# Low halves of weight tiles by an accumulating DMA instead of a VectorE subtraction

## The chip, the cores and the metric

The kernel runs on one core of one Trainium2 chip. The metric is the device time of one execution in microseconds. Three runs of the kernel before took 1213.09, 1211.47 and 1210.93 us; the median is 1211.47 us. In the profile the engines are called PE (TensorE), DVE (VectorE), ACT (ScalarE), POOL (GpSimd) and SP (SyncE, which issues most DMAs here).

## The reference

One decoder block on 512 tokens, to which 16 meta tokens are prepended (528 rows), with a model width of 1024:

```python
h = h + 0.5 * swiglu(rmsnorm(h, ffn1_norm), ffn1_w_gate, ffn1_w_up, ffn1_w_down)   # 1024 -> 2816 -> 1024
u = rmsnorm(h, mix_norm)
c_q, c_kv, k_rope, g_q, g_k, g_v, g_b, g_a, g_z, gate_mla, gate_gdn = split(u @ w_in)
y_mla = mla(c_q, c_kv, k_rope, ...) @ w_mla_o           # latent attention, 8 heads
y_gdn = gated_deltanet(g_q, g_k, g_v, ...) @ w_gdn_o    # short convolution, chunked delta rule
h = h + (sigmoid(gate_mla) * y_mla + sigmoid(gate_gdn) * y_gdn) @ w_out
h = h + 0.5 * swiglu(rmsnorm(h, ffn2_norm), ffn2_w_gate, ffn2_w_up, ffn2_w_down)
return rmsnorm(h, final_norm)[:, N_META:]
```

All of it is in float32.

## The kernel before, in words

**Products in halves.** PE multiplies in a reduced form of float32 (`fp32r`). To keep the precision, each operand is split into a high half, which is the value rounded to that form, and a low half, which is the difference. `mm3` (L182) makes a product of three passes: high weight by high data, high weight by low data, low weight by high data.

**Weight tiles.** `weights` (L178) and `wtiles` (L168) load a tile of 128 x 1024 float32 (512 KB; 128 x 768 for the down projection's last chunk) into `wraw` from SP's queue (3 buffers), cast it on ACT into `whi` (L173), and subtract on DVE into `wlo` (L174), 3 buffers each. There are 127 such tiles: 12 gate or up tiles of each feed-forward's first part, 24 down tiles (`wd`) of each, 36 of the mixer's projection (`win`), one for `ukv`, two for `uq`, and eight each of the merge's `mo` and `wo`.

**The two feed-forwards.** The first six column tiles of the gate and up matrices are multiplied directly ("gu", L188). The other 16 go in blocks of two by two with seven products instead of eight (`quad`, L405 and L421): their operands are sums of raw blocks (`sf`), each split on ACT and DVE into a `form` tile (L272, L273). Form tiles take their buffers in turn from the pools `whi`, `wlo` and `wex`. The hidden part is cut into three chunks of 8, 8 and 6 tiles; while a chunk is multiplied by the gate and up matrices, the down products ("dn") of the chunk before are put between the quads, so that down tile and seven sub-products alternate. The last chunk's eight down tiles follow one after another.

**The mixer** (374 to 764 us in the profile) has the projections, the triangular systems of the delta rule, the scan and the attention interleaved by slots (`At`), with eight heads of small matmuls. **The merge** multiplies by `mo` (gates applied on DVE, added on POOL as `sg`, L1326, then split on ACT and DVE into `mhl`, `mhA`, `mhD`) and then by `wo`. Feed-forward 2 and the last norm end the kernel.

**What sets the order.** The code is written in program order with priorities (`At`, `cur_priority`), and a scheduler with a model of costs sets the order of each engine's instructions; buffers of the pools and semaphores do the rest. Each engine, and each DMA queue's issuing engine, runs its instructions in that order.

Of the kernel before, what the change touches and what calls it, by code (L numbers as in the profile page):

```python
# [9 lines left out]
F32 = mybir.dt.float32  # L10
F32R = mybir.dt.float32r
AF = mybir.ActivationFunctionType
ALU = mybir.AluOpType
# [4 lines left out]
P = 128  # L18
# [4 lines left out]
KT = D // P  # L23
# [26 lines left out]
}.items() for n in ns.split()}  # L50
SOLVE = 16
M34 = 17.5
WLO = ()
LAG = 3
NC1 = 3
NC2 = 3
# [5 lines left out]
NSF = 3  # L62
ORD = (2, 0, 3, 1, 4, 5, 6, 7)
ONP = (2, 3)
NFORM = {"whi": 3, "wlo": 3, "wex": 2}
CYCLE = (0, 1, 2)
HOLD = (('nm', 0, 0, 32), ('nm', 1, 0, 36), ('b', 0, 1, 36), ('g', 0, 2, 42), ('tok', 1, 4, 5), ('tok', 2, 5, 4), ('tok', 3, 6, 2), ('back', 0, 8, 25), ('tok', 4, 8, 21), ('tok', 7, 10, 0), ('sq', 0, 11, 25), ('kvn', 0, 14, 12), ('kvn', 1, 14, 18))
GX = (1,) * 16
# [13 lines left out]
KW, VW, QW, MISC, CKV, CQ, ZW, GM, GG = 1, 5, 9, 0, 13, 14, 16, 20, 28  # L82
# [10 lines left out]
def build(tc, a, out, tap=None):  # L93
    nc = tc.nc
    ctx = ExitStack()
    tap = tap or (lambda name, ap: None)
    with ctx:
        cst = ctx.enter_context(tc.tile_pool(name="cst", bufs=1))
        wp = ctx.enter_context(tc.tile_pool(name="wp", bufs=3))
# [25 lines left out]
        def mm_tile(name):  # L125
            return mmp.tile([P, 2, 512], F32, tag="mm", name=name)
# [7 lines left out]
        def ax_tile(name):  # L134
            return smp.tile([P, 512], F32, tag="ax", name=name, bufs=1)

        table_ops, fence, last_split, trail, marks, tiles = [], [None], [], [], {}, {}

        def mark(name, i, ins):
            marks.setdefault((name, i), []).append(ins.ins)  # L140
# [18 lines left out]
        def halves(t):  # L159
            return t[:, :, 0:HALF]  # L160
# [4 lines left out]
        def v2(ap):  # L165
            return ap.rearrange("p (a b) -> p a b", a=2)

        def wtiles(src, n, pool_lo=0):  # L168
            raw = wp.tile([P, 8, P], F32, tag="wraw", name="wraw", bufs=3)
            hi = wp.tile([P, 8, P], F32R, tag="whi", name="whi")  # L170
            lo = wp.tile([P, 8, P], F32R, tag="wlo", name="wlo")
            nc.sync.dma_start(raw[:, 0:n], src)
            ih = nc.scalar.copy(hi[:, 0:n], raw[:, 0:n])  # L173
            il = (nc.gpsimd if pool_lo else nc.vector).tensor_tensor(out=lo[:, 0:n], in0=raw[:, 0:n], in1=hi[:, 0:n].bitcast(F32), op=ALU.subtract)  # L174
            last_split[:] = ih.ins, il.ins
            return hi, lo

        def weights(src, n, pool_lo=0):  # L178
            hi, lo = wtiles(src, n, pool_lo)
            return [(hi[:, i], lo[:, i]) for i in range(n)]  # L180

        def mm3(outs, ws, xs, start, stop):  # L182
# [9 lines left out]
        def outs528(ps):  # L192
            return [(ps[:, 0, 0:HALF], 0, HALF), (ps[:, 1, 0:HALF], HALF, NT)]
# [77 lines left out]
        def split(pool, x, hi, lo, eng=None):  # L271
            nc.scalar.copy(hi, x)  # L272
            (eng or nc.vector).tensor_tensor(out=lo, in0=x, in1=hi.bitcast(F32), op=ALU.subtract)  # L273
# [3 lines left out]
        def form(x, pool):  # L277
            tag = ("whi", "wlo", "wex")[CYCLE[cycle[0] % len(CYCLE)]]
            cycle[0] += 1
            t = (pool if tag == "wex" else wp).tile([P, 8, P], F32R, tag=tag, name="form", bufs=NFORM[tag])  # L280
            split(wp, x, t[:, 0:4], t[:, 4:8])
# [188 lines left out]
            for m in range(KT):  # L470
                down(len(CHUNKS) - 1, m)

        # ---------------- feed-forward 1
        xs = []
        with tc.tile_pool(name="hid", bufs=1) as hid, tc.tile_pool(name="fp", bufs=2) as fp:
            norm = Norm(fp, NT, "n1", None, nc.vector)
# [36 lines left out]
        tap("h1", h1d)  # L513


        # ---------------- token mixer
        gated = dr.tile([16, P, SEQ], F32, name="gated")
        zd = dr.tile([4, P, SEQ], F32, name="zd")
        yd = dr.tile([4, P, SEQ], F32, name="yd")
# [7 lines left out]
        win = a["win"]  # L527
# [15 lines left out]
        mixer = ExitStack()  # L543
# [5 lines left out]
        def tmp(name, n=SEQ, parts=P, dt=F32):  # L549
            tag = TAG[name]  # L550
            return mx.tile([P, NT + 3], dt, tag=tag, name=name, bufs=NTAG[tag])[0:parts, 0:n]
# [14 lines left out]

        def proj(t, name, n=NT, ax=False):
            with At(WPRI):
                w = weights(win[t], KT, t in WLO)
            if ax:  # L570
                ps = ax_tile(name)
                mm3([(ps, NM, NT)], w, us, True, True)
                return ps
            ps = mm_tile(name)
            trail.clear()
            if n == NT:
                mm3(outs528(ps), w, us, True, True)
                tiles[t] = list(trail)
                return halves(ps)
            mm3([(ps[:, 0, :], NM, NT)], w, us, True, True)  # L580
            tiles[t] = list(trail)
            return ps[:, 0, :]
# [22 lines left out]
        ktok = [tok("ktok") for c in range(5)]  # L605
        bv = [tok("bv") for c in range(5)]

        # ---- rates and decays, token-major
        def rates():
            ps = proj(MISC, "misc")  # L610
            nc.vector.tensor_tensor(out=v2(misc), in0=ps, in1=v2(r), op=ALU.mult)
# [86 lines left out]
                nc.vector.tensor_tensor(out=e1, in0=e1, in1=e2, op=ALU.add if x else ALU.subtract)  # L698
                dq.dma_start(krd[16 * x:16 * x + 16], e1)

        # ---- short convolution, token-major copies
        def conv_tile(t, ci, dst):
            ps = proj(t, "qkv")
            x = tmp("cx", NT + 3)
# [66 lines left out]
        def hs(tiles, h, lo_, hi_):  # L771
            return tiles[h // 2][64 * (h % 2):64 * (h % 2) + 64, lo_:hi_]

        # ---- the triangular systems
        def decay(c, lower, n):
            if lower:
                t = b4("dec", [P, H, P]) if c else one([NM, H, NM], "L0")
# [191 lines left out]
                nc.vector.tensor_tensor(out=zs, in0=ps, in1=zs, op=ALU.mult)  # L969
                dq.dma_start(yd[:, :, o - NM:o - NM + P].rearrange("i p t -> p i t"), zs)  # L970

        # ---- the compressed keys, values and queries
        ckvn, cqn = [], []
        cph, cpl = one([P, P], "cph", F32R), one([P, P], "cpl", F32R)

# [50 lines left out]

        def queries():
            with At(WPRI):
                wq = weights(a["uq"][:, 0:8], 8) + weights(a["uq"][:, 8:12], 4)
            ps = mm_tile("qr")  # L1030
            for x in range(2):
                mm3([(ps[:, x, :], 0, SEQ)], wq[8 + 2 * x:10 + 2 * x], cqn, True, True)
            cosq, sinq = tmp("cosq"), tmp("sinq")
            dq.dma_start(cosq, a["cosq"])
            dq.dma_start(sinq, a["sinq"])
            for x in range(2):
                e1, e2 = tmp("e1"), tmp("e2")
                nc.vector.tensor_tensor(out=e1, in0=ps[:, x, :], in1=cosq, op=ALU.mult)
                nc.vector.tensor_tensor(out=e2, in0=ps[:, 1 - x, :], in1=sinq, op=ALU.mult)
                nc.gpsimd.tensor_tensor(out=e1, in0=e1, in1=e2, op=ALU.add if x else ALU.subtract)  # L1040
                dq.dma_start(qrd[x], e1)
            for t in range(4):
                ps = mm_tile("qn")
                mm3([(ps[:, 0, :], 0, SEQ)], wq[2 * t:2 * t + 2], cqn, True, True)
                qn = tmp("qn")
                ecopy(EQ[t])(qn, ps[:, 0, :])
                dq.dma_start(qnd[t], qn)

        # ---- latent attention
        mS = one([P, NT + NM], "mS")  # L1050
        nb = one([P, H, 4], "nb")
        ls = one([P, H, 4], "ls")
# [110 lines left out]
        def gate_steps(js):  # L1163
            for j in js:
                with At(WPRI):
                    w = weights(win[GM + j], KT, GM + j in WLO)
                ps = ax_tile("gate")
                for k in range(KT):
                    mm3([(ps, NM, NT)], w[k:k + 1], us[k:k + 1], k == 0, k == KT - 1)
                    if k < KT - 1:  # L1170
                        yield
                t = tmp("gt")
                nc.vector.tensor_tensor(out=t, in0=ps, in1=r[:, NM:NT], op=ALU.mult)
                dq.dma_start(gated[j], t)
                yield
# [41 lines left out]
            for _ in gates:  # L1217
                pass

        # ---- emission; At(slot) sets the priority of a part  # L1220
        with At(0):
            rates()
        table_set(SILU)
# [27 lines left out]
        with At(10):  # L1251
            nc.vector.tensor_tensor(out=hd(bv[0][0:NM]), in0=psm[0:NM].rearrange("p c (h d) -> p (c h) d", d=64),
                                    in1=hb(beta[0:NM, 0], NM), op=ALU.mult)
# [48 lines left out]
        with At(60):  # L1302
            attention()

        # ---- merge
        table_set("sigmoid_and_others")
        tc.cur_priority = p0 + 200 * STEP
        yxs = []
# [6 lines left out]
        for m in range(KT):  # L1315
# [4 lines left out]
            w = weights(a["mo"][m], 8)  # L1320
# [14 lines left out]
        norm = Norm(mx, SEQ, "n2", True)  # L1335
# [11 lines left out]
        tap("h2", h2d)  # L1347
        mixer.close()

        # ---------------- feed-forward 2 and the last norm  # L1350
        with tc.tile_pool(name="hid2", bufs=1) as hid, tc.tile_pool(name="fp2", bufs=2) as fp:
            norm3 = Norm(fp, SEQ, "nf")
            h3 = []
# [120 lines left out]
```

## Time and profile before

| | |
|---|---|
| median of three runs | 1211.47 us (1210.93 to 1213.09) |
| span of the profiled execution | 1213.2 us |
| PE busy | 1182.6 us, 97% of the span |
| DVE busy | 857.0 us, 71% |
| ACT busy | 539.7 us, 44% |
| POOL busy | 127.1 us, 10% |
| HBM read, written | 126.47 MB, 17.55 MB |

The profile is of one execution; its span is the time from the first to the last instruction, and the busy times are sums over instructions of an engine. A busy PE is not PE at its peak, since matmuls overlap and their ends are modelled. "PEclk" is the granted TensorE clock, 1.00 for full speed. A row's bracket, as in [4.39 <-PE dn], is the time the engine was idle before it and what ended that time.

### The profile page before, as it was taken

The numbers are of one execution on the slowest core, as the hardware profiler recorded it, in microseconds if no ns is written. First come the engines' busy times: TensorE is split into PE (matmuls) and PEld (weight loads), VectorE is DVE, ScalarE is ACT, GpSimd is POOL, SyncE is SP. The second block draws the span as 40 slices with busy tenths as digits, with TensorE's granted clock in tenths as the row PEclk, the third lists the DMA queues.
The fourth block names the chain that finished last, engine by engine and source line by source line (L and its number), as shares of the span: only waits on it lengthen the run. The fifth ranks groups of instructions, "written<-read, shape, count | busy, mean of one in ns | idle before, by whom it ended". The sixth has DMA issues, their size and how long they took to land.

```text
span 1213.2 us, 20599 instructions
## 1 busy us (share of the span) xinstructions
PE 1182.6 (97%) x8094; PEld 1072.4 (88%) x8094; DVE 857.0 (71%) x1545; ACT 539.7 (44%) x922; POOL 127.1 (10%) x129
## 2 busy tenths in 40 slices
PE   7999999999999899999999999999999999999996
PEld 7999999999999789788897777788889999999985
DVE  7978777876656877784667665554979777786754
ACT  6544334533345553254425564434536433543443
POOL 1000000000011545020400000222000000000002
PEclk9999999999999888898999999999999999999998
DMA  6433233232244322245534544554642233233222
GB/s 233 143 103 100 94 105 105 88 118 75 88 138 138 126 61 81 81 145 149 162 101 142 173 132 135 169 185 141 199 157 88 90 103 104 94 106 115 79 78 70
DMA packets 68961, 145.37 MB, mean 120 GB/s; under 512 B 20000, under 2 KB 26480, under 8 KB 68864
## 3 DMA queue, kind: packets, MB, share of 16 engines
q1 hardware_dynamic: 68320, 143.52, 37.0%
q8 instruction: 64, 1.05, 0.3%
q10 hardware_dynamic: 544, 0.52, 0.1%
q14 instruction: 33, 0.27, 0.1%
HBM read 126.47 MB, written 17.55 MB: 119 GB/s over the span
## 4 chain that ended last, share of the span: by engine, by line
PE 86%; DVE 5%; issue 3%; POOL 2%; ACT 2%; DMA 2%; SPq 0%; DVEq 0%; POOLq 0%; ACTq 0%
PE gu L405 27%; PE dn L188 21%; PE gu L188 11%; PE gate L188 6%; PE wo L188 4%; PE mo L188 3%; PE qkv L188 2%; DVE wlo L174 1%; PE kk L804 1%; PE s L1085 1%; PE s L1082 1%; PE qk L943 1%; POOL rk L827 1%; DVE rk L827 1%; DVE T L829 1%
## 5 line engine op out<-in xcount | busy, mean ns | idle before, releaser
L173 ACT CAST whi<-wraw 128x1024 fp32r<-128x1024 f32 (+1 forms) x127 | 129.2, 1017 | 195.6 <-issue 65.3
L174 DVE TENSOR_TENSOR wlo<-wraw,whi 128x1024 fp32r<-128x1024 f32 (+1 forms) x127 | 155.8, 1227 | 26.2 <-ACT whi L173 25.5
L405 PE MATMUL gu<-hd,form 128*128 128x264 f32 (+1 forms) x1152 | 154.6, 283 | 0.0
L405 PEld LDWEIGHTS gu<-hd,form 128*128 128x128 f32 x1152 | 146.6, 190 | 1.3
L272 ACT CAST form<-sf 128x512 fp32r<-128x512 f32 x128 | 78.6, 620 | 126.1 <-DVE sf L394 67.5
L323 DVE SCALAR_TENSOR_TENSOR hk<-dn,hk 128x528 f32<-128x528 f32 (+2 forms) x49 | 33.7, 688 | 109.8 <-PE dn L188 109.6
L405 PE MATMUL gu<-ut,form 128*128 128x264 f32 x768 | 101.1, 284 | 0.0
L405 PE MATMUL gu<-rb,form 128*128 128x256 f32 x768 | 100.0, 283 | 0.0
L188 PE MATMUL dn<-hd,whi 128*128 128x264 f32 (+2 forms) x366 | 97.4, 319 | 0.0
L272 ACT CAST form<-wraw 128x512 fp32r<-128x512 f32 x96 | 59.3, 620 | 85.2 <-PE gu L405 52.1
L405 PEld LDWEIGHTS gu<-ut,form 128*128 128x128 f32 x768 | 96.5, 188 | 0.0
L405 PEld LDWEIGHTS gu<-rb,form 128*128 128x128 f32 x768 | 95.6, 192 | 0.0
L273 DVE TENSOR_TENSOR form<-sf,form 128x512 fp32r<-128x512 f32 x128 | 86.9, 683 | 11.2 <-ACT form L272 11.1
L188 PE MATMUL gate<-ut,whi 128*128 128x512 f32 x256 | 87.8, 417 | 0.0
L188 PE MATMUL dn<-ra,whi 128*128 128x264 f32 x464 | 85.3, 285 | 0.0
L188 PE MATMUL dn<-ut,whi 128*128 128x512 f32 (+1 forms) x238 | 83.6, 390 | 0.0
L235 POOL TENSOR_TENSOR sqa<-sq 128x512 f32<-128x512 f32 (+1 forms) x3 | 4.5, 1514 | 674.3 <-ACT sq L222 674.3
L188 PE MATMUL gu<-ra,whi 128*128 128x264 f32 x384 | 64.5, 290 | 7.4 <-ACT whi L173 6.6
L188 PE MATMUL dn<-ra,wlo 128*128 128x264 f32 x352 | 71.6, 285 | 0.0
L188 PE MATMUL dn<-ut,wlo 128*128 128x512 f32 (+1 forms) x182 | 70.4, 387 | 0.0
L273 DVE TENSOR_TENSOR form<-wraw,form 128x512 fp32r<-128x512 f32 x96 | 65.5, 684 | 6.7 <-ACT form L272 6.4
L188 PEld LDWEIGHTS dn<-ra,whi 128*128 128x128 f32 x464 | 68.5, 189 | 0.0
(435 smaller groups left out, 2480.7 us busy)
## 6 DMA issues: line engine op xcount, KB each, us to landing
wraw<-w SPq DMA_DIRECT2D x88, 512.0 KB, 3.3
wraw<-win SPq DMA_DIRECT2D x36, 512.0 KB, 3.5
wraw<-d SPq DMA_DIRECT2D x32, 512.0 KB, 3.8
wraw<-d SPq DMA_DIRECT2D x16, 384.0 KB, 3.2
hk<-xT SPq DMA_DIRECT2D x16, 264.0 KB, 3.6
dec<-growd SPq DMA_DIRECT2D x8, 512.0 KB, 5.8
gated<-gt SPq DMA_DIRECT2D x16, 256.0 KB, 2.2
sg<-gated SPq DMA_DIRECT2D x16, 256.0 KB, 2.8
```

The costliest lines, as they stand in the source:

```text
L173: ih = nc.scalar.copy(hi[:, 0:n], raw[:, 0:n])
L174: il = (nc.gpsimd if pool_lo else nc.vector).tensor_tensor(out=lo[:, 0:n], in0=raw[:, 0:n], in1=hi[:, 0:n].bitcast(F32), op=ALU.subtract)
L188: trail.append(nc.tensor.matmul(o, lhsT=w, rhs=x[:, lo_:hi_], start=start and k == 0 and pi == 0, stop=stop and k == n - 1 and pi == 2).ins)
L272: nc.scalar.copy(hi, x)
L273: (eng or nc.vector).tensor_tensor(out=lo, in0=x, in1=hi.bitcast(F32), op=ALU.subtract)
L323: nc.vector.scalar_tensor_tensor(out=o, in0=p, scalar=0.5, in1=o, op0=ALU.mult, op1=ALU.add)
L405: nc.tensor.matmul(ps, lhsT=wt, rhs=xt, start=k == 0 and i == 0, stop=k == 3 and i == 2)
L804: nc.tensor.matmul(ps[0:n, h4, 0:n], lhsT=hs(kT, h, o, o + n), rhs=hs(kT, h, o, o + n), start=True, stop=True)
L827: eng.tensor_tensor(out=tm, in0=lt[:, m + 1:m + 1 + n, m:m + 1].broadcast_to([nl, n, m + 1]), in1=T[:, m:m + 1, 0:m + 1].broadcast_to([nl, ...
L829: eng.tensor_tensor(out=T[:, m + 1:m + 1 + n, 0:m + 1], in0=T[:, m + 1:m + 1 + n, 0:m + 1], in1=tm, op=ALU.subtract)
L943: nc.tensor.matmul(ps[:, h4], lhsT=hs(kT, h, o, o + n), rhs=hs(qT, h, o, o + n), start=True, stop=True)
L1082: nc.tensor.matmul(ps[:, 0:w], lhsT=Q[h][:, b * P:(b + 1) * P], rhs=K[h][:, k0:k1], start=True, stop=True)
```

## The change

Two ways of making a tile now stand beside each other. `wtiles` is as before. In `wtiles_dma` ACT makes the high half and, in a second pass, its negative into the buffer of the low half; then POOL issues a DMA from the same place in HBM that `wraw` was loaded from, with an addition, so that the low half becomes raw minus high. The first five tiles of the program (`NEARLY`), those of `win` and `uq` (`own`), and `ukv`, which calls `wtiles` itself, stay with DVE; 83 tiles take the new path: 31 in feed-forward 1 (7 gate or up, 24 down), 16 in the merge and 36 in feed-forward 2 (12 and 24). `whi` has 4 buffers instead of 3, and `wlo` 5. The size of the scratch for DMAs whose descriptors the core itself writes is set to 4096. Names that nothing used, and comments, go.

```diff
-WLO = ()
+OWN = True
-NFORM = {"whi": 3, "wlo": 3, "wex": 2}
+NFORM = {"whi": 4, "wlo": 5, "wex": 2}
+NEARLY = 5
...
+        nw = [0]
...
-        def wtiles(src, n, pool_lo=0):
+        def wtiles(src, n):
...
-            il = (nc.gpsimd if pool_lo else nc.vector).tensor_tensor(out=lo[:, 0:n], in0=raw[:, 0:n], in1=hi[:, 0:n].bitcast(F32), op=ALU.subtract)
+            il = nc.vector.tensor_tensor(out=lo[:, 0:n], in0=raw[:, 0:n], in1=hi[:, 0:n].bitcast(F32), op=ALU.subtract)
...
-        def weights(src, n, pool_lo=0):
-            hi, lo = wtiles(src, n, pool_lo)
+        def wtiles_dma(src, n):
+            raw = wp.tile([P, 8, P], F32, tag="wraw", name="wraw", bufs=3)
+            hi = wp.tile([P, 8, P], F32R, tag="whi", name="whi", bufs=NFORM["whi"])
+            lo = wp.tile([P, 8, P], F32R, tag="wlo", name="wlo", bufs=NFORM["wlo"])
+            nc.sync.dma_start(raw[:, 0:n], src)
+            nc.scalar.copy(hi[:, 0:n], raw[:, 0:n])
+            nc.scalar.activation(lo[:, 0:n], hi[:, 0:n].bitcast(F32), AF.Copy, scale=-1.0)
+            nc.gpsimd.dma_start(lo[:, 0:n], src, accum_op=ALU.add)
+            return hi, lo
+
+        def weights(src, n, own=False):
+            hi, lo = (wtiles if own or nw[0] < NEARLY else wtiles_dma)(src, n)
+            nw[0] += 1
             return [(hi[:, i], lo[:, i]) for i in range(n)]
...
-                w = weights(win[t], KT, t in WLO)
+                w = weights(win[t], KT, OWN)
...
-                wq = weights(a["uq"][:, 0:8], 8) + weights(a["uq"][:, 8:12], 4)
+                wq = weights(a["uq"][:, 0:8], 8, True) + weights(a["uq"][:, 8:12], 4, True)
...
-                    w = weights(win[GM + j], KT, GM + j in WLO)
+                    w = weights(win[GM + j], KT, OWN)
...
-    nc = bacc.Bacc("TRN2", target_bir_lowering=False, num_devices=1)
+    nc = bacc.Bacc("TRN2", target_bir_lowering=False, num_devices=1, dynamic_dma_scratch_size=4096)
```

ACT at the first quad of feed-forward 1 that has a down tile ahead of it; `g` is the gate's activation, `whi` the down tile's high half, `p` the copy of the quad's first product. Before:

```order
L147 ACTIVATE g<-g 128x528
L272 CAST form<-sf 128x512
L272 CAST form<-wraw 128x512
L421 COPY p_1486<-gu 128x264
L173 CAST whi<-wraw 128x1024
L272 CAST form<-wraw 128x512 x2
L272 CAST form<-sf 128x512 x4
```

Now:

```order
L149 ACTIVATE g<-g 128x528
L185 CAST whi<-wraw 128x1024
L186 ACTIVATE wlo<-whi 128x1024
L434 COPY p_1494<-gu 128x264
L285 CAST form<-wraw 128x512 x2
L285 CAST form<-sf 128x512
```

The cast of the down tile has moved ahead of the copy `p`, and the negation into `wlo` stands right behind it; the copy and the casts of the forms come after both.

POOL from the end of the attention (`of` is its last multiplication for a block of queries) into the merge (`sg` is the sum of the two gated branches of tile 0, 1, 2, ...). Before:

```order
L1157 TENSOR_TENSOR of<-of,rl 128x512
L1108 MEMSET vf 32x64 x2
L1157 TENSOR_TENSOR of<-of,rl 128x512 x2
L1326 TENSOR_TENSOR sg_8503<-sg_8503,sg_8504 128x512
L1326 TENSOR_TENSOR sg_8546<-sg_8546,sg_8547 128x512
```

Now:

```order
L1170 TENSOR_TENSOR of<-of,rl 128x512
L187 DMA wlo<-mo 128x1024 x3
L1170 TENSOR_TENSOR of<-of,rl 128x512
L187 DMA wlo<-mo 128x1024
L1339 TENSOR_TENSOR sg_8534<-sg_8534,sg_8535 128x512
L187 DMA wlo<-mo 128x1024
L1339 TENSOR_TENSOR sg_8578<-sg_8578,sg_8579 128x512
L187 DMA wlo<-mo 128x1024
L1339 TENSOR_TENSOR sg_8622<-sg_8622,sg_8623 128x512
```

The DMAs for the tiles 0 to 3 of `mo` stand ahead of the first sum, and from there one DMA stands behind each sum: that of tile 4 behind the sum of tile 0, and so on into `wo`, with the DMA of `wo`'s third tile between the last two sums.

PE in the later part of the mixer (`v` and `kn` are products of the latent keys and values, `gate` a projection, `z` and `x` the small products of the triangular systems). Before:

```order
L1022 MATMUL v<-wlo,ckh 128x512
L188 MATMUL gate<-ut,whi 128x512 x2
L188 MATMUL gate<-ut,wlo 128x512
L188 MATMUL gate<-ut,whi 128x512 x2
L188 MATMUL gate<-ut,wlo 128x512
L188 MATMUL gate<-ut,whi 128x512
L864 MATMUL z_6671<-xt,dec 32x32 x32
L1022 MATMUL v<-whi,ckh 128x512
```

Now:

```order
L1035 MATMUL v<-wlo,ckh 128x512
L877 MATMUL z_6702<-xt,dec 32x32 x32
L201 MATMUL gate<-ut,whi 128x512
L201 MATMUL gate<-ut,wlo 128x512
L201 MATMUL gate<-ut,whi 128x512
L1035 MATMUL v<-whi,ckh 128x512
```

The 32 small products `z` follow the product `v` at once, and the gate's matmuls come behind them, three at a time between the products.

## Rows read from the trace of the kernel before

**Rows 1.** The page, busy time, share and instructions of each engine.

```profile
PE 1182.6 (97%) x8094; PEld 1072.4 (88%) x8094; DVE 857.0 (71%) x1545; ACT 539.7 (44%) x922; POOL 127.1 (10%) x129
```

**Rows 2.** Stretches: length, each engine's busy time, PEclk, DMA share, GB/s.

```profile
23.00:81.00 58.00, 58.00 (x482) 57.97 (x481) 50.22 (x85) 29.29 (x48) 0.00 (x0) 1.00 0.39 127
81.00:327.00 246.00, 246.00 (x2023) 246.00 (x2022) 189.28 (x338) 102.81 (x167) 0.00 (x0) 1.00 0.31 97
...
374.00:764.00 390.00, 377.16 (x2558) 321.25 (x2557) 260.79 (x548) 177.54 (x357) 76.73 (x90) 0.95 0.40 124
763.60:803.40 39.80, 39.80 (x171) 32.17 (x172) 23.33 (x28) 17.47 (x24) 12.63 (x7) 1.00 0.53 164
803.40:848.10 44.70, 44.70 (x194) 35.96 (x193) 21.16 (x25) 17.02 (x24) 12.83 (x7) 1.00 0.50 167
848.10:916.00 67.90, 67.90 (x297) 55.05 (x296) 56.03 (x92) 33.19 (x53) 0.00 (x0) 1.00 0.48 159
916.00:1155.00 239.00, 239.00 (x1679) 223.95 (x1679) 186.09 (x334) 102.78 (x167) 0.00 (x0) 1.00 0.32 100
```

**Rows 3.** PE's waits, the two longest: us in all, times, longest.

```profile
PE gu L188 <- ACT whi L173: 6.6, 1, 6.6
PE tok L723 <- ACT kT L147: 5.7, 1, 5.7
```

**Rows 4.** The chain of waits in feed-forward 1: start, length, work.

```profile
127.98 5.85 PE dn L188 x48
133.83 10.22 PE gu L405 x84
...
326.74 46.94 PE dn L188 x384
```

**Rows 5.** Groups by line and shape: busy, mean ns, idle before.

```profile
L174 DVE TENSOR_TENSOR wlo<-wraw,whi 128x1024 fp32r<-128x1024 f32 x110 | 139.1, 1265 | 26.2 <-ACT whi L173 25.5 <-PE qkv L188 0.3
...
L174 DVE TENSOR_TENSOR wlo<-wraw,whi 128x768 fp32r<-128x768 f32 x16 | 15.3, 955 | 0.0
...
L173 ACT CAST whi<-wraw 128x768 fp32r<-128x768 f32 x16 | 13.4, 836 | 41.4 <-PE dn L188 28.4 <-issue 6.6 <-PE gu L405 6.5
...
L147 ACT ACTIVATE dec<-dec 128x1024 f32<-128x1024 f32 x8 | 8.2, 1051 | 5.0 <-POOL dec L783 5.0
```

**Rows 6.** The timeline of one steady period, 148 to 163 us.

```profile
149.70 1.05 ACT L173 CAST whi<-wraw 128x1024 fp32r<-128x1024 f32 x1 [4.39 <-PE dn L188]
150.78 1.23 DVE L174 TENSOR_TENSOR wlo<-wraw,whi 128x1024 fp32r<-128x1024 f32 x1
...
155.85 0.62 ACT L272 CAST form<-wraw 128x512 fp32r<-128x512 f32 x1 [2.31 <-PE gu L405]
...
160.45 0.40 PE L188 MATMUL dn<-ra,wlo 128*128 128x264 f32 x2
```

**Rows 7.** DMA: a queue's packets, MB, share; issues' count, KB, us to landing.

```profile
q1 hardware_dynamic: 68320, 143.52, 37.0%
...
wraw<-d SPq DMA_DIRECT2D x32, 512.0 KB, 3.8
...
dec<-growd SPq DMA_DIRECT2D x8, 512.0 KB, 5.8
```

**Rows 8.** The timeline between the merge's two projections.

```profile
804.99 2.04 POOL L1326 TENSOR_TENSOR sg<-sg,sg 128x512 f32<-128x512 f32 x1 [3.39 <-DVE sg L1325]
...
808.46 0.19 PEld L188 LDWEIGHTS wo<-mhl,whi 128*128 128x128 f32 x1 [0.36 <-DVE mhl L273]
```

**Rows 9.** The later mixer: two stretches as in rows 2, and one timeline row.

```profile
480.00:570.00 90.00, 85.74 (x614) 72.10 (x613) 65.41 (x131) 39.10 (x66) 14.13 (x20) 0.91 0.36 115
550.00:560.00 10.00, 10.00 (x82) 8.14 (x82) 5.66 (x8) 4.95 (x11) 0.00 (x0) 0.55 0.34 119
...
547.90 2.11 PE L864 MATMUL z<-xt,dec 32*32 32x32 f32 x64 [0.38 <-DVE xt L856]
```

More of the change, by code (lines that the diff above doesn't have):

```diff
@@ L166, in v2 @@
             return ap.rearrange("p (a b) -> p a b", a=2)
-        def wtiles(src, n, pool_lo=0):
+        def wtiles(src, n):
             raw = wp.tile([P, 8, P], F32, tag="wraw", name="wraw", bufs=3)
-            hi = wp.tile([P, 8, P], F32R, tag="whi", name="whi")
-            lo = wp.tile([P, 8, P], F32R, tag="wlo", name="wlo")
+            hi = wp.tile([P, 8, P], F32R, tag="whi", name="whi", bufs=NFORM["whi"])
+            lo = wp.tile([P, 8, P], F32R, tag="wlo", name="wlo", bufs=NFORM["wlo"])
             nc.sync.dma_start(raw[:, 0:n], src)
             ih = nc.scalar.copy(hi[:, 0:n], raw[:, 0:n])
-            il = (nc.gpsimd if pool_lo else nc.vector).tensor_tensor(out=lo[:, 0:n], in0=raw[:, 0:n], in1=hi[:, 0:n].bitcast(F32), op=ALU.subtract)
+            il = nc.vector.tensor_tensor(out=lo[:, 0:n], in0=raw[:, 0:n], in1=hi[:, 0:n].bitcast(F32), op=ALU.subtract)
             last_split[:] = ih.ins, il.ins
             return hi, lo
-        def weights(src, n, pool_lo=0):
-            hi, lo = wtiles(src, n, pool_lo)
+        def wtiles_dma(src, n):
+            raw = wp.tile([P, 8, P], F32, tag="wraw", name="wraw", bufs=3)
+            hi = wp.tile([P, 8, P], F32R, tag="whi", name="whi", bufs=NFORM["whi"])
+            lo = wp.tile([P, 8, P], F32R, tag="wlo", name="wlo", bufs=NFORM["wlo"])
+            nc.sync.dma_start(raw[:, 0:n], src)
[6 more added lines that the diff above has]
+            nw[0] += 1
             return [(hi[:, i], lo[:, i]) for i in range(n)]
```

## The prediction

> **What bounds the kernel now.** I read the busy shares first. The PE row shows 97% of the span, DVE 71%, ACT 44% and POOL 10% [rows 1]; a lighter DVE helps only where PE waits for it. The stretches show where PE is at its limit: it is busy for the whole of 23 to 81 us and 81 to 327 us (feed-forward 1), of the two projections of the merge, and of the second feed-forward, and the granted clock is 1.00 there. In 374 to 764 us (the mixer) it is busy 377.16 of 390.00 us at 0.95 [rows 2]. Whatever time can be won beyond PE's own work lies in the mixer: 12.84 us idle and about 0.05 x 390 = 19.5 us of clock.
>
> The list of PE's waits comes next. The two longest are 6.6 us for the first high half at the start and 5.7 us for kT in the mixer [rows 3]; none of its 13 lines names a low half, which is what the change replaces. The chain of waits repeats it: in a steady period of feed-forward 1 a down tile holds PE 5.85 us and seven sub-products 10.22 us, 16.07 us together, one after the other, with no other engine between them [rows 4].
>
> **What is removed, added and moved.** 127 weight tiles are split before. 83 change path: 31 in feed-forward 1 (7 gate or up tiles after the first five, 24 down), 16 in the merge, 36 in feed-forward 2. Of the 83, 16 are the 768-wide down tiles of the last chunks, 67 are 1024 wide.
>
> *DVE* loses 67 x 1.265 + 16 x 0.955 = 84.8 + 15.3 = 100.0 us [rows 5]: 857 becomes about 757 us, 62%. On PE's path none of this lies, so I count it at 0.
>
> *ACT* gains one pass for each. The nearest operation of the same kind, size and engine is the activation on dec, 1.051 us; for 768 columns I take the cast, 0.836 us [rows 5]. 67 x 1.051 + 16 x 0.836 = 83.8 us, so 540 becomes about 624 us, 51%. What stands behind it on ACT is the next p copy and the casts of the forms, 1.05 us later. In the steady period ACT idles 2.31 us, waiting for a buffer that PE still reads, before the cast at 155.85 [rows 6]; this takes the delay up. If that cover were gone in each of the 32 periods with such a tile (16 in each feed-forward), the price would be at most 32 x 1.05 = 34 us; none of PE's 13 waits names a form, so I take 0.
>
> *SP's queue* keeps all its loads. The raw tile is free after ACT's cast and no longer after DVE's pass, 1.26 us sooner (150.75 against 152.01 [rows 6]); its next load starts so much sooner, which nobody waits for. *POOL* gets 83 issues; in the feed-forward's quads it has no work of its own, 0.00 us in 81 to 327 [rows 2]. *DMA* has 83 more reads of the same weights: 67 x 0.524 + 16 x 0.393 = 41.4 MB, on 143.52 MB [rows 7].
>
> **The new wait: low half by DMA.** In the steady period the high half is cast from 149.70 to 150.75, DVE's low half is ready at 152.01, and PE wants it at 160.45 [rows 6]: 8.44 us early. Now the negation ends at about 151.80 and 8.65 us are left for issue and landing. No DMA issued by POOL and no accumulating one is in this trace, so both parts need bounds. Landing: 3.8 us, as the plain load of the same 512 KB for a down tile, up to 5.8 us, the longest median of a 512 KB transfer (dec) [rows 7]. Issue on POOL: 0 up to 2.04 us, a whole pass of POOL over half such a tile [rows 8]. The sum is 3.8 to 7.84 us, and 0.8 to 4.9 us of the 8.65 stay. I take the nearer row, 3.8, and 1 us for the issue; the cost to PE is 0 at either end.
>
> In the dense phases there is no quad between tiles, but the high half has four buffers instead of three, so that a tile may be cast three tiles ahead. The shortest tile is the 768-wide one: 46.94 us / 384 matmuls = 0.122 us, times 36, 4.40 us [rows 4]. Three of these are 13.2 us; less cast and negation (0.84 each), 11.5 us are left for the DMA. In the merge a tile takes 39.80 / 171 x 24 = 5.59 us, so more.
>
> **POOL's queue in the merge.** From the order of POOL, the DMA for the low half of mo tile m + 4 stands behind the addition sg of tile m, in order. For the last tile it ends at 807.03 [rows 8], 3.6 us after the tile's matmuls, which end with the stretch at 803.4 [rows 2]; tile m + 4 starts three tiles, 16.8 us, after tile m ends, so 13 us are left for issue and landing. The other way, POOL's work waits for issues. The one addition without slack is the last: PE waits 0.36 us for the product made from it, at 808.46 [rows 8]. One issue stands between sg 6 and sg 7, but POOL idles 3.39 us ahead of sg 7, so an issue of up to that is hidden. On the other side, DVE's low half that ran beside sg 7 is gone, which can bring back at most 0.36 us. I take 0.
>
> **DMA engines.** 143.52 MB in 37.0% of 1213.2 us is 320 GB/s with all engines busy [rows 1, 7], so a 512 KB tile is 1.64 us of all 16. In a steady period the share goes from 0.31 to (0.31 x 16.07 + 1.64) / 16.07 = 0.41. In the first projection of the merge it goes from 0.53 x 39.8 = 21.1 us by 7.1 tiles x 1.64 = 11.7 to 32.8 of 39.8 us; in the second from 22.4 by 13.1 to 35.5 of 44.7; at the start of feed-forward 2 from 0.48 x 67.9 = 32.6 by 12 tiles, 19.7, to 52.3 of 67.9 [rows 2]. It fits, at 0.77 to 0.83. The cost is 0 as long as the accumulating transfer costs the engines what a plain one costs.
>
> **The mixer.** Its projections stay on the old path. Up to about 480 us the order of DVE, ACT and PE is that of before. After that PE's order differs. The 32 small matmuls z of the last merging step before the scan's end, which waited 0.38 us for DVE's transpose xt at 547.90 [rows 9], stood behind seven gate matmuls and now stand ahead of them, while two others have come before: five matmuls at 44.70 / 194 = 0.23 us [rows 2], so z comes 1.2 us sooner and waits as much longer. That sum is 0 to +1.5 us; the last weights' earlier loads can return as much. I take 0 +- 2.
>
> **Sum.** 0 from the feed-forwards and merge, 0 +- 2 from the mixer. The rows are of an execution with a span of 1213.2 us; the median of the three runs is 1211.47 and the highest 1213.09, so the profiled one lies 1.7 us above the median. From the median: 1211 us, own range 1208 to 1214. A change of under 0.2%, 2.4 us, can't be told from none.
>
> **A rule that speaks against it.** First the row: a plain 512 KB tile costs 1.64 us of engine time, worked out above [rows 7]. The Trainium skill, "Collectives: The Full Stack", section "The bandwidth ceiling: the fold count and why AG ≠ RS ≠ AR", states that a DMA that adds has to read two sources, with two read descriptors for each piece, and moves at half the rate for that (62.28 against 32.35 GB/s there). No transfer of this trace adds, so the rows neither bear it out nor refute it. By that rule the time would be that of rival 2.
>
> **Rivals.**
>
> 1. *Faster, through the mixer.* The stretch from 480 to 570 us loses 4.26 us to idle PE and 0.09 x 90 = 8.1 us to the lower clock; in 550 to 560 alone the granted clock is 0.55 on average, so most of it passes at 1.2 and not at 2.4 GHz, and 4.5 us go there [rows 9]. It begins right behind PE's wait at 547.90. If the new order takes PE past this place without a gap, 4.5 us of clock and about 1.5 us of the idle time return: 1211 - 6 = 1205 us. For it: exactly this place is rearranged. Against: z is put earlier against its operand, not later.
>
> 2. *Slower, the DMA engines become the bound in the merge.* If an accumulating tile takes twice the engine time, the sums above become 21.1 + 23.3 = 44.4 us against 39.8, 22.4 + 26.2 = 48.6 against 44.7, and 32.6 + 39.4 = 72.0 against 67.9: +4.6, +3.9, +4.1, together 12.6 us, and 1211 + 13 = 1224 us. It decides from 1.6 times on, (39.8 - 21.1) / 11.7. In the steady periods even twice is only (5.0 + 3.3) / 16.07 = 0.52. For it: the merge is the one place with PE full and DMA over 0.5. Against: only if it is really the engines and not the memory that a share shows.
>
> 3. *Slower, through the mixer.* z waits longer for xt than the gate matmuls covered, and the idle is followed by one more stretch at the lower clock: 1.5 + 4.5 = +6, less what the old one cost if it moves only; +4, 1215 us.
>
> 4. *Slower, the DMA comes late in every period*, if issue and landing take over 8.65 us. At 10 us, 32 x 1.35 = 43 us: 1254 us. It needs twice the 4.8 us that I take, and more than the 7.84 of my upper bounds.
>
> 5. *The change doesn't do what it says.* If the tiles stayed with DVE, DVE would keep 857 us and the time 1211; the order shows the ACTIVATE and the DMA for each tile, so I give this nothing.
>
> **How the numbers follow.** Forecast 0.37. Rival 1 gets 0.32: a rearranged mixer moves its clock either way, and the one trace has over 8 us to win there against a place that is already near its work. Rival 2 gets 0.13: no row shows such a transfer, and its factor may lie on either side of 1.6. Rival 3 gets 0.14, as the mirror of rival 1 with less behind it; rival 4 0.04, as it lies beyond both bounds. Faster by over 0.2%: 0.32; within: 0.37; slower: 0.31. The range reaches 1204 below, past rival 1, and 1222 above, past rival 3 and into the lower part of rival 2 (a factor of 1.8); the rest of rival 2, rival 4 and a stronger rival 1 are left out, about 0.2.
>
> **What would show it.** After: DVE about 757, ACT about 624 us; PE's waits without a line for a low half in a feed-forward; a period still of 16.07 us; accumulating transfers landing in 4 to 6 us; DMA share 0.41 in the steady part and about 0.8 in the merge; the mo and wo rows of PE as long as before. Wrong: PE waiting for wlo after a DMA (rival 2 or 4), told apart by whether it is in the merge or in each period; or a time off by over 3 us with the difference between 480 and 764 us (rivals 1 and 3).

## The result, and the profile after

The changed kernel took 1220.52 us (median of four runs, 1219.15 to 1225.66); the ratio to the kernel before is 1.0078, with a 95% interval of 1.0055 to 1.0101: slower by 0.8%, 9 us. I had said 1211 us and no measurable change. The profiled execution has a span of 1223.9 us, 10.7 more than before's.

The busy shares of the changed kernel, to be put beside [rows 1]:

```profile
PE 1181.3 (97%) x8094; PEld 1068.9 (87%) x8094; DVE 772.5 (63%) x1462; ACT 613.8 (50%) x1005; POOL 192.5 (16%) x212
```

PE has the same work, DVE is 84 us lighter, ACT 74 us heavier. Its DMA queues (packets, MB, share of 16 engines) and issues, to [rows 7]:

```profile
q1 hardware_dynamic: 68320, 143.52, 36.3%
q0 software_dynamic: 11952, 41.42, 20.2%
...
wraw<-d SPq DMA_DIRECT2D x32, 512.0 KB, 3.7
wlo<-d POOLq DMA_DIRECT2D x32, 512.0 KB, 5.9
...
sg<-gated SPq DMA_DIRECT2D x16, 256.0 KB, 3.9
```

The new queue q0 moves 41.42 MB in 20.2% of 1223.9 us, 247 us of all 16 engines: 5.97 us for a MB, against 444 / 143.52 = 3.10 for the plain transfers of q1 (36.3% of the span is 444 us). By this an addition costs the engines 1.93 times a plain transfer of q1, 3.1 us for a 512 KB tile where I had 1.64.

The period of the steady part is as forecast. The chain of one period, and the timeline behind it:

```profile
160.30 5.85 PE dn L201 x48
166.15 10.22 PE gu L418 x84
```

```profile
165.94 1.05 ACT L185 CAST whi<-wraw 128x1024 fp32r<-128x1024 f32 x1 [4.98 <-PE dn L201]
167.03 1.06 ACT L186 ACTIVATE wlo<-whi 128x1024 fp32r<-128x1024 f32 x1
168.38 0.87 POOL L187 DMA_DIRECT2D wlo<-d  x1 [21.88 <-ACT p L434]
```

The period is 16.07 us as in [rows 4]. The landing is the time from a transfer's issue to the arrival of its last part. Issued at 168.38, the low half lands at 174.3 by the median of 5.9, and PE wants the tile at 176.7.

The loss stands in two stretches. These rows answer to the three of [rows 2] that begin at 763.60, 803.40 and 848.10:

```profile
764.00:808.00 44.00, 40.31 (x167) 31.93 (x166) 12.32 (x21) 23.21 (x31) 14.95 (x14) 0.96 0.81 204
808.00:852.50 44.50, 44.50 (x194) 36.07 (x193) 12.46 (x18) 24.86 (x32) 15.76 (x15) 1.00 1.02 282
852.50:926.30 73.80, 70.65 (x295) 56.61 (x293) 47.45 (x86) 42.15 (x64) 7.86 (x9) 0.95 0.79 217
```

And these are two of PE's waits that the view of [rows 3] did not have:

```profile
PE mo L201 <- DVE sg L1338: 3.7, 2, 2.2
PE gu L201 <- ACT form L285: 3.1, 1, 3.1
```

In the part of mo, PE idles 3.7 us and runs at 0.96 of its clock; in the part of wo, where the DMA share is 1.02, it loses nothing; at the start of feed-forward 2 it idles 3.1 us and loses as much again to the clock. The lower clock stands right behind the last idle of each: 0.57 from 796 to 800 us and 0.50 from 907 to 911, so PE runs there for the most part at 1.2 and not at 2.4 GHz. From each profile I read three lengths: the mixer from the last down product of feed-forward 1 to the first mo matmul, the merge from there to the last of wo, and the start of feed-forward 2 from there to the first quad. Before they are 384.6, 89.9 and 67.6 us; now 382.3, 96.2 and 73.8. With 0.4 us before the mixer and 0.1 behind, 0.4 - 2.3 + 6.3 + 6.2 + 0.1 = 10.7 us, the whole difference of the spans.

What holds up mo is seen in the chain of the changed kernel (start, length, work; a q behind an engine's name is its sequencer, which waits and issues):

```profile
777.76 5.08 DMA sg<-gated
782.87 0.02 ACTq L149
782.93 0.04 ACT sg L149
783.07 0.02 ACTq L185
783.47 1.04 ACT wlo L186
784.51 0.52 ACT mhl L285
785.05 0.70 DVE mhl L286
785.77 5.11 DMA sg<-gated
```

This is a circle. ACT's order puts the sigmoid of the gates of tile m + 4 and the negation ahead of `mhl`, the cast of tile m + 1. The cast has its operand but has to wait, in ACT's order, until the gates of tile m + 4 have landed. When it and DVE's part are done, a gate buffer is free and the next load starts, and lands 5.1 us later. One turn is 785.77 - 777.76 = 8.0 us, and PE needs 5.6 for a tile. In the kernel before the same order stands on ACT, but the casts come at PE's pace:

```profile
767.97 0.62 ACT L272 CAST mhl<-sg 128x512 fp32r<-128x512 f32 x1 [2.77 <-POOL sg L1326]
773.43 0.60 ACT L272 CAST mhl<-sg 128x512 fp32r<-128x512 f32 x1
779.24 0.62 ACT L272 CAST mhl<-sg 128x512 fp32r<-128x512 f32 x1 [0.38 <-POOL sg L1326]
```

The gate loads from 764 to 808 us land in 2.9 us before and in 5.1 in the changed kernel (the rows before and after, in this order):

```profile
sg<-gated SPq DMA_DIRECT2D x8, 256.0 KB, 2.9
sg<-gated SPq DMA_DIRECT2D x8, 256.0 KB, 5.1
```

Before, landing, sigmoid, cast and DVE's part add up to 2.9 + 0.6 + 0.6 + 0.7 = 4.8 us, within the 5.6. The 2.2 us of later landing and the 1.0 of the negation make it 8.0.

### The profile page after: what moved, and what is told of

It is laid out like the page before. It is cut to its first block, busy times and chain, and to the rows that moved or that the text cites. A ratio compares the mean times of both kernels' runs of the same rounds, so it can differ in the third digit from the quotient of the medians.

```text
span 1223.9 us, 20734 instructions
## 1 busy us (share of the span) xinstructions
PE 1181.3 (97%) x8094; PEld 1068.9 (87%) x8094; DVE 772.5 (63%) x1462; ACT 613.8 (50%) x1005; POOL 192.5 (16%) x212
## 3 DMA queue, kind: packets, MB, share of 16 engines
q1 hardware_dynamic: 68320, 143.52, 36.3%
q0 software_dynamic: 11952, 41.42, 20.2%
## 4 chain that ended last, share of the span: by engine, by line
PE 81%; DVE 6%; DMA 5%; issue 3%; POOL 2%; ACT 2%; SPq 0%; DVEq 0%; POOLq 0%; ACTq 0%
PE gu L418 27%; PE dn L201 20%; PE gu L201 10%; PE gate L201 6%; PE wo L201 4%; PE qkv L201 2%; DMA wraw<-w 2%; DMA sg<-gated 1%; PE mo L201 1%; DVE wlo L176 1%; PE s L1098 1%; PE s L1095 1%; PE z L201 1%; DVE T L842 1%; DVE rk L840 1%
## 5 line engine op out<-in xcount | busy, mean ns | idle before, releaser
L187 POOL DMA_DIRECT2D wlo<-d x48 | 42.0, 875 | 537.8 <-ACT wlo L186 203.3
L186 ACT ACTIVATE wlo<-whi 128x1024 fp32r<-128x1024 f32 (+1 forms) x83 | 84.3, 1015 | 1.7
L407 DVE TENSOR_TENSOR sf<-wraw 128x512 f32<-128x512 f32 x64 | 44.0, 688 | 48.4 <-DMA wraw<-w 48.1
```

What stands on the lines that cost most here:

```text
L186: nc.scalar.activation(lo[:, 0:n], hi[:, 0:n].bitcast(F32), AF.Copy, scale=-1.0)
L187: nc.gpsimd.dma_start(lo[:, 0:n], src, accum_op=ALU.add)
L407: nc.vector.tensor_tensor(out=t, in0=x, in1=y, op=op)
```

## The experiments

All are edits of the changed kernel, profiled and timed against the kernel before on the same chip. The stages of their profiles, in us, with the ratio of times and its 95% interval:

| kernel | mixer | merge | start of ffn 2 | median | ratio to before |
|---|---|---|---|---|---|
| before | 384.6 | 89.9 | 67.6 | | |
| changed | 382.3 | 96.2 | 73.8 | 1220.52 | 1.0078 (1.0055 to 1.0101) |
| e1 merge and start by DVE | 381.3 | 89.8 | 67.6 | 1212.49 | 1.0005 (0.9985 to 1.0025) |
| e2 plain copy | 380.1 | 90.6 | 67.8 | 1214.86 | 1.0015 (0.9993 to 1.0036) |
| e3 negation on DVE | 382.9 | 95.2 | 74.4 | 1227.91 | 1.0147 (1.0117 to 1.0176) |
| e4 all by DVE | 385.1 | 89.8 | 67.6 | 1213.58 | 1.0017 (0.9996 to 1.0038) |
| e5 mo by DVE | 381.4 | 89.6 | 67.8 | 1213.40 | 1.0019 (0.9995 to 1.0044) |
| e6 merge by DVE | 380.3 | 89.9 | 70.3 | 1213.07 | 1.0023 (1.0001 to 1.0045) |
| e7 start by DVE | 379.7 | 94.1 | 67.6 | 1217.03 | 1.0046 (1.0027 to 1.0064) |
| e8b projections by DMA | 389.9 | 89.9 | 67.6 | 1224.66 | 1.0096 (1.0064 to 1.0127) |
| e11 gates by DMA | 380.8 | 89.9 | 67.6 | 1211.43 | 1.0003 (0.9989 to 1.0016) |
| e13 plain and a spare copy | 380.2 | 94.2 | 73.8 | 1221.38 | 1.0077 (1.0049 to 1.0105) |
| e14 wo and start by DVE | 385.7 | 101.5 | 67.6 | 1222.89 | 1.0080 (1.0055 to 1.0106) |
| e15 cast first | 385.1 | 90.9 | 67.8 | 1216.47 | 1.0023 (0.9999 to 1.0046) |
| e16 e14, cast first | 379.1 | 90.9 | 67.6 | 1214.47 | 1.0018 (0.9994 to 1.0041) |

**Undo it where it loses (e1).**

```diff
-            w = weights(a["mo"][m], 8)          # likewise wo, and gate and up tiles where n == SEQ
+            w = weights(a["mo"][m], 8, True)
```

> The changed kernel, but the 16 tiles of the merge (mo, wo) and the 12 gate and up tiles at the start of feed-forward 2 are made by DVE again; 55 tiles (31 in feed-forward 1, 24 down in feed-forward 2) keep the accumulating DMA. Theory A (the accumulating transfer holds the DMA engines about twice as long per byte, and raw, gate and residual loads come late where PE was full and the DMA share was above 0.45): the waits of PE for sg (3.7 us) and for a form (3.1 us) go, the time is 1208 to 1212 us. Theory B (ACT's extra pass in the merge delays the gates): the same, since these passes go too. Theory C (the new order in the mixer, the buffers or POOL's queue elsewhere): it stays at 1217 to 1221 us.

1212.49 us; both waits are gone. The loss is in these 28 tiles; the 55 others, all in the other parts of the feed-forwards, cost and bring nothing that is clear of the interval.

**A plain copy (e2), and the negation on DVE (e3).**

```diff
-            nc.gpsimd.dma_start(lo[:, 0:n], src, accum_op=ALU.add)
+            nc.gpsimd.dma_start(lo[:, 0:n], src)                      # e2
```
```diff
-            nc.scalar.activation(lo[:, 0:n], hi[:, 0:n].bitcast(F32), AF.Copy, scale=-1.0)
+            nc.vector.tensor_scalar(out=lo[:, 0:n], in0=hi[:, 0:n].bitcast(F32), scalar1=-1.0, scalar2=None, op0=ALU.mult)   # e3
```

> The changed kernel with POOL's DMA as a plain copy instead of an addition: it leaves out the subtraction of the high half, so the low half holds the raw weight. Bytes from HBM, POOL issues, ACT passes and the order of every engine stay. Theory A: the share of POOL's queue falls from 20.2% of the span to 10 to 12%, the DMA share in wo from 1.02 to about 0.8, the waits for sg and form in the merge and feed-forward 2 go or fall under 1 us, the time is 1209 to 1213 us. Theory B (ACT) and theory C (order, POOL's queue): it stays at 1217 to 1221 us.

> The changed kernel with the negation on DVE instead of ACT; the accumulating DMA stays for all 83 tiles. Theory A: DMA shares as in the changed kernel, 1216 to 1223 us. Theory B: ACT is relieved by 84 us and the merge by 16 passes of 1.05 us, so the time falls to 1209 to 1213 us. Theory C: 1217 to 1221 us.

With the plain copy 1214.86 us and with DVE's negation 1227.91, so ACT's time alone is not what is lost; why e3 is slower still was not taken apart. The queue of e2:

```profile
q0 software_dynamic: 11952, 41.42, 11.8%
```

The same bytes take 143 us of the engines, 3.45 a MB. In its circle a gate load lands in 4.5 us, and the merge loses only 0.7. The circle is too slow here as well: the first four casts `mhl` start at 762.99, 771.40, 779.19 and 785.80, 22.8 us for three tiles that take PE 16.8. That is 6.0 us too long, and PE waits 0.3 us for sg. In the changed kernel they start at 766.05, 776.41, 784.41 and 792.45, 9.6 us too long, and PE waits 3.7. In e7 below it is 7.5 and 1.8. So PE works some 6 us ahead of the gates; it waits for what goes beyond that, and the clock adds its part.

**Parts of it (e5, e6, e7, e14).** Each makes some of mo, wo and the start of feed-forward 2 by DVE, with the edit of e1: e6 mo and wo, e7 the start, e5 mo, e14 wo and the start.

> The changed kernel with only the 16 merge tiles (mo, wo) by DVE again; the start of feed-forward 2 keeps its 12 accumulating DMAs. Theory A in the form that the merge hands a backlog on to feed-forward 2: without it feed-forward 2's start needs 32.6 + 12 x 3.1 = 70 us of all DMA engines in 67.9, so it loses 0 to 3 us instead of 6.2, and the time is 1209 to 1214 us. Theory A without a backlog: the start of feed-forward 2 still loses 6 us, 1215 to 1217 us. Theory C: 1217 to 1221 us.

> The changed kernel with only the 12 gate and up tiles at the start of feed-forward 2 by DVE again; the 16 merge tiles keep the accumulating DMA. Theory A (DMA engines): the merge keeps its loss against the kernel before (PE waits for sg, some 4 to 6 us from the first mo matmul to the last of wo), the start of feed-forward 2 takes 67 to 70 us instead of 73.8, and the time is 1214 to 1219 us. Theory A' (the merge alone is the cause and its backlog reaches feed-forward 2 whatever is made there): 1218 to 1221 us.

> The changed kernel with only the eight mo tiles by DVE again; wo and the start of feed-forward 2 keep the addition. By the sum of engine time (3.1 us for a tile) wo's part needs 22.4 + 8 x 3.1 = 47 of 44.7 us and the start of feed-forward 2 70 of 67.9: no waits for sg, a merge of 89.9 to 91 us, a start of 70 to 73 us (2.7 of its own and what wo hands on), and 1213 to 1217 us. If the loss sat in mo's tiles alone: merge 90, start 67.6 to 70.3, 1210 to 1213 us. If each part loses for itself however little is put on the engines: 1218 to 1221 us.

> The changed kernel with the additions of feed-forward 1, of mo and of feed-forward 2's down tiles only; wo and the start of feed-forward 2 by DVE. If mo's eight additions alone keep back the loads of sg: PE waits for sg 2 us or more, a merge of 92 to 96 us, start 67.6, 1213 to 1218 us. If the merge's loss needs wo's additions too, whose raw loads and additions are issued while mo still runs: merge 89.8 to 91 us, 1209 to 1213 us.

In these kernels the merge loses where mo's tiles are added by DMA and nowhere else. The start of feed-forward 2 loses 6 us and more only in kernels that load all three parts, 2.7 with its own additions alone (e6) and 0.2 with wo's as well (e5), so that its loss is not a sum of tiles by price; by engine time e5 should have lost some 5 us in wo and the start, and lost none. And e14 spoke against full engines: with only mo's eight additions the merge lost most of all, 11.6 us, at a share of 0.73. Its stretch:

```profile
764.00:808.00 44.00, 38.58 (x156) 29.75 (x155) 13.79 (x20) 19.70 (x26) 12.09 (x10) 0.96 0.73 185
```

Its waits of PE:

```profile
PE mo L201 <- DVE sg L1338: 4.2, 3, 2.1
...
PE wo L201 <- ACT mhl L285: 1.9, 1, 1.9
```

**Engine time without an addition (e10, e12, e13).** The plain copy of e2 and a second one: e10 into the same tile, e12 into HBM, e13 of the high half into HBM.

```diff
-            nc.gpsimd.dma_start(lo[:, 0:n], src, accum_op=ALU.add)
+            nc.gpsimd.dma_start(lo[:, 0:n], src)
+            spare = dr.tile([P, 8, P], F32R, tag="spare", name="spare", bufs=4)
+            nc.gpsimd.dma_start(spare[:, 0:n], hi[:, 0:n])             # e13; e12 reads src, e10 writes lo again
```

> The changed kernel with two plain copies of each tile in place of the one accumulating DMA: it leaves out the subtraction, as the single plain copy did, and issues 166 DMAs from POOL instead of 83. If what costs is engine time, about two plain transfers per tile, then the share of POOL's queue is 20 to 24% as with the addition, the merge takes 93 to 98 us instead of the 90.6 of the single copy, the start of feed-forward 2 70 to 76 instead of 67.8, and the time is 1217 to 1226 us. If it is something of the addition itself (its order after the negation, its reading back of SBUF), the merge stays below 92 us and the time at 1210 to 1215 us.

> The changed kernel with a plain copy into the low half, as in the single plain copy (it leaves out the subtraction), and a second plain copy of the same 83 tiles into HBM that nobody reads. Unlike the two copies into one tile, no transfer stands behind another for the low half, so only engine time and POOL's issues are added. If twice the engine time is what the addition costs: POOL's queue at 19 to 24% of the span, a merge of 93 to 98 us and a start of feed-forward 2 of 70 to 76 us, 1217 to 1226 us. If engine time doesn't matter: merge 90 to 91 us, start 67.8, 1210 to 1215 us.

> The changed kernel with a plain copy into the low half (it leaves out the subtraction) and a second plain copy, of the tile's high half from SBUF to HBM, which nobody reads and which can't start before the high half is made; so it runs beside the tile's other transfers, in the merge too. Engine time for a tile is then near that of the addition (some 3 us of all 16). If engine time is what costs: DMA share of 0.95 or more in the merge, the landing of sg from 3.7 us (single copy) to 4.5 or more, a merge of 93 to 98 us, a start of feed-forward 2 of 70 to 76, and 1216 to 1225 us. If it is the addition itself: merge 90 to 91 us, start 67.8, 1210 to 1215 us.

e10 missed its question: the second copy into a tile waits for the first, so the low half came two landings late (PE waits 31.8 us for it in the down products), 1294.12 us. e12 missed too: its spare copies wait only for one another, and POOL issued all 83 in the first 177 us; 1246.59 us, with a share of 0.94 to 1.00 there, and a merge of 89.6. e13 answered: 94.2 and 73.8, so 4.3 of the merge's 6.3 us and all of the start's loss, with no addition in it. Its time is not to be compared: feed-forward 1 ends 3.6 us later than before. Its stretches:

```profile
764.00:808.00 44.00, 41.29 (x176) 32.71 (x176) 13.77 (x23) 24.71 (x31) 16.69 (x21) 1.00 0.93 309
808.00:852.50 44.50, 44.50 (x194) 35.91 (x193) 12.68 (x18) 25.01 (x33) 17.69 (x23) 1.00 1.07 374
```

**Open the circle (e15, e16).** The cast of tile m + 1 goes ahead of the sigmoid of tile m + 4 in ACT's order; every transfer stays.

```diff
                 table(sg[j], sg[j], AF.Sigmoid)
+                if m >= 4:
+                    behind(table_ops[-1], casts[m - 3])
...
-            split(mx, sg[0], mh, ml)
+            casts.append(nc.scalar.copy(mh, sg[0]).ins)
+            nc.vector.tensor_tensor(out=ml, in0=sg[0], in1=mh.bitcast(F32), op=ALU.subtract)
```

> The changed kernel, all 83 additions in place, but in the merge ACT takes the cast of tile m + 1 (mhl) ahead of the sigmoid of tile m + 4, so that the load of the next gate no longer waits for the landing of this one. If the circle is the merge's loss: no waits of PE for sg, a merge of 89.8 to 91 us instead of 96.2, the start of feed-forward 2 still near 74, and 1213 to 1217 us. If the loss is the engines' time as such: merge 94 to 97, 1218 to 1223 us.

> The kernel with mo's additions only in the merge and at the start of feed-forward 2 (DVE for wo and the gate and up tiles), with the same order of cast and sigmoid. If the circle is the loss: merge 89.8 to 91 us instead of 101.5, start 67.6, 1209 to 1213 us. If not: 1218 to 1224 us as without it.

The merge falls from 96.2 to 90.9 us and from 101.5 to 90.9, with no wait for sg. Of e15's 0.23% above the kernel before, the merge and the start account for 1.2 us; the rest is not clear of the interval. The casts on ACT in the timeline of e15, and its gate loads:

```profile
774.38 0.62 ACT L1347 CAST mhl<-sg 128x512 fp32r<-128x512 f32 x1 [0.79 <-POOL sg L1341]
...
779.98 0.62 ACT L1347 CAST mhl<-sg 128x512 fp32r<-128x512 f32 x1 [0.80 <-POOL sg L1341]
...
sg<-gated SPq DMA_DIRECT2D x8, 256.0 KB, 7.0
```

Its stretches:

```profile
755.00:800.00 45.00, 43.94 (x189) 35.03 (x188) 15.04 (x23) 28.23 (x36) 15.15 (x15) 1.00 0.98 251
800.00:845.00 45.00, 45.00 (x196) 36.45 (x195) 12.94 (x19) 24.91 (x32) 15.73 (x15) 1.00 1.00 264
845.00:919.00 74.00, 74.00 (x328) 60.12 (x327) 49.93 (x90) 45.19 (x68) 10.07 (x11) 1.00 0.83 232
```

The casts are at PE's pace again, 5.60 us apart, though a gate load now lands in 7.0 us. The share is 0.98 and 1.00 for 90 us, and none of PE's waits names a load or an sg. A share is the time of the packets, and it reached 1.07 in e13, so 1.00 does not prove that the engines could carry no more.

The start of feed-forward 2 is back at 67.8 too, which I had not expected: the 6 us are lost only behind a merge that ran late. What its profile shows goes by the landing of the raw loads there. These are the rows of before and of the changed kernel, and PE's wait in e6:

```profile
wraw<-w SPq DMA_DIRECT2D x11, 512.0 KB, 3.3
wraw<-w SPq DMA_DIRECT2D x11, 512.0 KB, 8.4
PE gu L201 <- ACT form L285: 2.2, 1, 2.2
```

In e2, e5 and e15 they land in 5.6, 6.8 and 7.1 us and the start loses 0.2 at most; in e6 in 7.9, and it loses 2.7; in e13 and the changed kernel in 8.2 and 8.4, and it loses 6.2. From e6 to the changed kernel PE's wait grows only from 2.2 to 3.1 us; the rest is the clock, 1.00 in e6 and 0.95 in the changed kernel.

**HBM or the engines, buffers alone, the mixer (e9, e4, e8b, e11).** e9 adds from the raw tile in SBUF (`raw[:, 0:n]` for `src`); e4 sets `NEARLY = 127`; e8b sets `OWN = False` and e11 drops `OWN` at the gates, both on top of e1.

> The changed kernel with the accumulating DMA reading the raw tile that already lies in SBUF instead of the weight in HBM: 41.4 MB less are read from HBM. If the DMA engines are the limit (theory A), the share of POOL's queue stays at 18 to 21% and the time at 1217 to 1225 us, or above, since the raw buffers are free later. If it is HBM's bandwidth, the loads of raw and sg in the merge land as before the change (3.7 and 2.8 us) and the time falls to 1209 to 1214 us.

> The changed kernel with all 127 tiles by DVE: no accumulating DMA, no negation, but four and five buffers and what these do to the order. If the mixer's gain (the first mo matmul 1.9 us sooner than before, in the profile of the changed kernel) comes from the buffers and the order, it is here too: 1208 to 1211 us. If it comes from what the DMA takes off DVE at the mixer's edges, the time is that of before, 1211 to 1213.5 us.

> The merge and the start of feed-forward 2 by DVE, and the 36 tiles of the mixer's projections by the accumulating DMA, which the changed kernel leaves to DVE; feed-forward 1 and the down tiles of feed-forward 2 as changed. If DVE's low halves hold up the mixer (11 of its pieces of over 1 us stand in the chain of waits, among them one of 2.84 us ahead of kT, for which PE waits 5.7 us), and the DMA share there, 0.32 to 0.52, leaves room for 36 x 3.1 = 112 us of 390, the time falls to 1203 to 1209 us. If the transfers, landing in 6 to 8 us in place of 1.3 us of DVE, come too late for the projections, or hold back the loads of heads and decays, it rises to 1214 to 1225 us.

> The merge and the start of feed-forward 2 by DVE, of the mixer's projections the first 20 by DVE too, and only the 16 gate tiles by the accumulating DMA. With all 36 the mixer took 389.9 us against 384.6 before. If the loss came from the early projections (PE waits for kT and ktok there, DVE and POOL are both on the chain), the late gates cost nothing and 20 us less DVE work may show: mixer 378 to 384 us, 1206 to 1212 us. If it came from DMA engines shared with the loads of decays, zs and heads, the mixer is again above 386 us, 1214 to 1220 us.

e9 took 1231.77 us, 1.0162 (1.0137 to 1.0186), with q0 at 18.3%, a merge of 97.0 and a start of 77.8: reading less from HBM helps nothing, and the raw buffers, held until the addition has landed, hold up the next loads (SP's queue waits 364 us in all for such landings). e4 is within 0.4% of before: buffers and order alone bring nothing clear. In e8b the mixer is 389.9 us, longest of all, and with the gates alone (e11) 380.8. So it is the early projections that lose by it, as far as one profile of each can tell; the late ones don't show. No version beats the kernel before beyond its interval.

## Why the prediction was wrong

- **DVE, ACT, POOL.** Right in size for what was changed. The groups of the low half on DVE shrank by 99.5 us (100.0 forecast), the negations are 84.3 us (83.8), an issue on POOL takes 0.87 us (1 taken). The engines as a whole moved less, to 772.5 and 613.8 us where I had 757 and 624: neighbouring rows of an engine overlap in the timelines, and its busy time counts the overlap once. No PE time hung on them in the feed-forwards' steady periods.
- **The new wait in the steady period.** Right: PE waits for no low half. The landing is 5.9 us, just above my upper bound of 5.8 and not the 3.8 that I took; for wo it is 8.5, beyond my range, and still nobody waits for it. The DMA share of the steady part is 0.50, not 0.41.
- **DMA engines: the step that failed.** I wrote: "It fits, at 0.77 to 0.83. The cost is 0 as long as the accumulating transfer costs the engines what a plain one costs." With that the merge and the start of feed-forward 2 stood at 0 in my sum; they lost 6.3 + 6.2 = 12.5 us. The condition doesn't hold: a MB costs 1.93 times the transfers of q1, and 1.73 times the plain copy of the same tiles by the same queue (5.97 to 3.45, e2). The Trainium skill's "Collectives: The Full Stack", section "The bandwidth ceiling: the fold count and why AG ≠ RS ≠ AR", says of the reduce step of a collective that its add needs two source reads, and has half the rate for it, 62.28 to 32.35 GB/s. The trace agrees in size, for a DMA within one core: 5.97 to 3.10 us a MB.
- **And what the step asked was the wrong question.** I compared the engines' time with the length of each stretch. e15 has a share of 0.98 and 1.00 there and loses 1.0 us. What was due was to follow each load that lands later to the one that waits for it. The list of DMA issues of the kernel before has the gate loads (2.8 us), and the sigmoid ahead of `mhl` on ACT could be read from the order; the circle had 5.6 us for landing, sigmoid, cast and DVE, and took 4.8 of them. I followed POOL's queue in the merge and not ACT's, where the negation stands in the circle as well (1.04 of the 8.0 us).
- **Rival 2** named the right place and nearly the size, 12.6 us against 12.5 in the merge and the start. That the sums agree is luck. Its terms are not borne out: 3.9 us forecast for wo, where nothing was lost, and a limit by capacity that e15 refutes. The wide range up to 1222 us took in the measured time for this rival and rival 3, not for the circle.
- **The mixer.** 2.3 us shorter in this one profile. Over all kernels with the same mixer tiles it lies between 378.5 and 385.7 us without relation to the edits, so the forecast of 0 +- 2 can't be told from chance. Rivals 1 and 3 are neither needed nor excluded.
- **Left open.** Why the raw loads of the start land later behind a late merge, and why the clock falls there and not in e6, was not taken apart further. In the changed kernel's chain one raw load, issued at 893.41, takes 11.2 us, and PE waits 3.1 us for the form made from it.

## What to carry to other kernels

A DMA that takes work off an engine can be paid for in the landing time of other loads; here that of the gates went from 2.9 to 5.1 us. So look for loads that close a circle: buffer free, load, an operation in an in-order queue, and behind it the operation that frees the next buffer. Such a circle has to be summed and compared with the pace of the bounding engine, and reordering two instructions in it can be worth more than the transfers: here a cast ahead of a sigmoid gave back 5 of the merge's 6 us with all transfers in place. A stage can also hide a slow circle for a while: e2's was 6.0 us behind after three tiles and cost 0.7.

## What the runs showed of the hardware

An accumulating DMA into SBUF takes 5.97 us of all 16 engines for a MB, a plain one from the same queue 3.45 (e2), the plain transfers of the other queue 3.10. From SBUF to SBUF the addition costs hardly less, 0.183 x 1231.6 / 41.42 = 5.44 us (e9). Sixteen engines at a share of 0.98 to 1.00 over 90 us cost PE 1.0 us where the order left room (e15), and one of 0.73 cost 11.6 where it left none (e14). POOL's issue of an accumulating DMA takes 0.87 us, of a plain one 0.54 (e2).
